# Half-size matmuls of linear attention, head norms and differential scores written as full 128x128 forms

## The chip, the cores and the metric

The kernel runs on one core of one Trainium2 chip. The metric is the device time of one execution in microseconds (us), the median of three runs. A core has a matrix engine (TensorE, PE in the profile, with its weight loads as PEld), VectorE (DVE), ScalarE (ACT), GpSimd (POOL), and SyncE (SP), which issues most of the DMA transfers here. TensorE reads a stationary operand of up to 128 rows (the contraction) and 128 columns (which become the partitions of the result) and streams a moving operand of up to 512 columns through it. A matmul whose contraction has 64 rows, or whose stationary operand has 64 or 32 columns, is called half-size in this text, one of 128 x 128 full.

## The reference, cut to what matters

Two layers of a diffusion backbone on 256 context tokens and 256 latent tokens, 1024 features. In each layer one projection of the normalised input feeds three branches: (A) grouped-query attention with a norm of every head of 64 features, (B) a bidirectional gated linear attention in chunks of 64 tokens, (C) differential attention. Their outputs go through gates into one projection; a gated MLP with a short convolution follows. The second layer gives no context output.

```python
# A: norm of each head of 64 features
qa_l = apply_axial_rope(rms_norm(qa_l, qk_g[0]), cos, sin) * scale
# B: chunks of 64 tokens, once forward and once backward
att = jnp.where(causal, jnp.einsum('bhnid,bhnjd->bhnij', q_d, k_d), 0.0)
o_intra = jnp.einsum('bhnij,bhnje->bhnie', att, v)
o_inter = jnp.einsum('bhncd,bhnde->bhnce', q_d, s_start)
# C: two softmaxes over heads of 64 features
sc = jnp.einsum('bqhmd,bkhmd->bhmqk', qc, kc).astype(jnp.float32)
pc = jax.nn.softmax(sc, axis=-1)
pd = (pc[:, :, 0] - lam * pc[:, :, 1]).astype(vc.dtype)
```

## The kernel before

All large products run on float32 operands split into two halves of the type float32r, a high and a low one; a product is three matmuls (high x high, high x low, low x high). Weights come by DMA into tiles `raw`; ScalarE casts the high half `wh` (L336), VectorE makes the low half `wl` (L338), three tiles of each in rotation. Projections are L350 to L352 (feature-major) and L562 to L564 (token-major), outputs of the MLP and of the branches' sum L467 to L469.

Functions are written as streams: a lead stream (linear attention, then attention A, then C) is woven with a fill stream (values, gates, merges, and in layer 0 the sums L266 of the conditioning) by costs that each step yields. From that the framework makes a fixed order for every engine; each engine works through its own order, and waits where an operand or a buffer is not ready. Two pools of PSUM banks hold results: three `mm` for projections, five `ps` for the rest.

*Values* (`vproj`, L550): 1184 columns in four blocks of 296, for four tiles of 128 tokens, into one tile `V`: the values of B, the decay input, the values of A and of C. Blocks 1 and 0 come ahead of the linear attention, blocks 2 and 3 in its fill.

*Linear attention* (`gla`, L797): for context and latent tokens (g) and four heads (h), 16 passes, of which 12 want an output (all in layer 0, the latent ones in layer 1). The 64 features of a head lie twice on the partitions, forward in 0 to 63, backward in 64 to 127. A pass makes cumulative decays `G` (L850), chunk sums `us` (L856, contraction over the 64 tokens of a chunk), exponentials `ep` and `en` on ScalarE, `en` times the keys on GpSimd (L865), `qd` = `ep` times the queries on VectorE (L867), and then the scores `at` (L876, contraction over 64 features, forward and backward apart), which are masked and added to `as`. The states `ss` are carried from chunk to chunk on VectorE (L894), after GpSimd has cleared or copied their start (L884 to L888). The output `o` of a tile of 128 tokens is one full matmul of `as` with the values (L901) and two of `qd` with a state (L903), each for 64 tokens, so 64 columns of the stationary operand. A norm follows, whose power is GpSimd's (L364). Operands here are float32, not float32r; a float32 matmul leaves two records in the trace.

*Head norms of A* (`head_scale`, L581, ten calls): squares on ScalarE, per token tile a matmul with 32 columns of ones (L587), a copy of its rows (L589), a transposition (L591), and the mean (L593).

*Scores of C* (`attention_c`, L679): a score is two matmuls into one bank. `stacked` (L482) puts the high half of a key head on its 64 partitions and the low half on the other 64; `doubled` (L492) puts the high half of a query head on both. The first matmul contracts over all 128 partitions (high query with both key halves), the second over 64 (low query with high key). Then come the maximum (L723), the exponential (L598), and the difference of the two softmaxes (L732) on VectorE and ScalarE, transpositions (L516) and the product with the values (L700). The scores of A (`attention_a`) are two full matmuls each, of the same shapes.

The functions that the change touches, and what calls them:

## Time and profile before

| | |
|---|---|
| three runs, us | 1602.23, 1603.44, 1605.70 |
| median, us | 1603.44 |
| profiled execution: first to last instruction, us | 1602.8 |
| TensorE busy, us (share) | 1544.4 (96%) |
| VectorE busy | 1018.0 (64%) |
| ScalarE busy | 744.7 (46%) |
| GpSimd busy | 221.7 (14%) |

The profile is one execution. For the profiled execution only its span is known, 0.6 us below the median of the runs. TensorE's busy time has modelled ends: neighbouring matmuls overlap in it, and one of 128 columns shows a duration of 0.27 us though the next may start 0.11 us later. Starts are what can be compared. The chain of work that ended last, and the waits, name TensorE for nearly all of the run. Layer 0 has its linear attention at about 100 to 205 us, attention A to 358, attention C to 530; in layer 1 these stages stand at 1085 to 1170, to 1260, and to 1350.

### The profile page before, as it was taken

To read this page: it belongs to the slowest core of one execution; us is meant where nothing else is said; L and a number is where in the kernel's file an instruction comes from. 1 tells how busy PE (TensorE), PEld (TensorE's weight loads), DVE (VectorE), ACT (ScalarE), POOL (GpSimd) and SP (SyncE) were. 2 spreads that over 40 slices of the span, in tenths; PEclk is the share of its full clock that TensorE was granted. 3 is DMA by queue.
4 is the path that set the end of the run, shared out by engine and by line. 5 is a ranking of instruction groups with operands and counts; after the bars stand their busy time and mean duration, and the time that the engine had idled before them with its cause. 6 is when DMAs were issued, how large, how long until landed. Compare 5 with 4: busy or idle time off the path is not lost. (4 is left out here: it accounts for less than half of the span.)

```text
span 1602.8 us, 25470 instructions
## 1 busy us (share of the span) xinstructions
PE 1544.4 (96%) x9859; PEld 1279.6 (80%) x9859; DVE 1018.0 (64%) x1963; ACT 744.7 (46%) x1330; POOL 221.7 (14%) x284
## 2 busy tenths in 40 slices
PE   7999999999999998999999999899999999899998
PEld 4898767776777887988788777799888878799986
DVE  3636554555667546877787845646667687577754
ACT  3464334453444346533333335655545655465543
POOL 2101110000111223100000223610111122200000
PEclk8999999999999999999999999999999999999999
DMA  9421245215422346644455545432333223665553
GB/s 318 146 88 49 78 149 154 73 54 169 140 60 72 111 134 218 186 149 147 147 157 162 162 128 162 139 109 74 113 125 106 72 74 113 215 205 182 183 191 110
DMA packets 91577, 217.28 MB, mean 136 GB/s; under 512 B 7568, under 2 KB 34832, under 8 KB 91456
## 3 DMA queue, kind: packets, MB, share of 16 engines
q1 hardware_dynamic: 90496, 212.37, 42.2%
q0 software_dynamic: 960, 3.29, 0.7%
q8 instruction: 77, 1.26, 0.3%
q14 instruction: 44, 0.36, 0.1%
HBM read 214.58 MB, written 1.05 MB: 135 GB/s over the span
## 5 line engine op out<-in xcount | busy, mean ns | idle before, releaser
L338 DVE TENSOR_TENSOR wl<-raw,wh 128x1024 fp32r<-128x1024 f32 (+4 forms) x333 | 385.2, 1161 | 223.2 <-ACT wh L336 218.7
L336 ACT CAST wh<-raw 128x1024 fp32r<-128x1024 f32 (+4 forms) x333 | 320.7, 967 | 305.5 <-PE mm L351 146.0
L350 PE MATMUL mm<-act,wh 128*128 128x256 f32 (+1 forms) x1096 | 376.1, 343 | 0.8 <-DVE ft L990 0.7
L352 PE MATMUL mm<-act,wl 128*128 128x256 f32 (+1 forms) x1096 | 371.3, 339 | 1.3 <-DVE wl L338 1.2
L351 PE MATMUL mm<-act,wh 128*128 128x256 f32 (+1 forms) x1096 | 371.1, 339 | 0.4 <-POOL act L398 0.4
L350 PEld LDWEIGHTS mm<-act,wh 128*128 128x128 f32 x1096 | 208.6, 190 | 28.5 <-issue 8.2
L352 PEld LDWEIGHTS mm<-act,wl 128*128 128x128 f32 x1096 | 208.6, 190 | 25.8 <-issue 2.7
L351 PEld LDWEIGHTS mm<-act,wh 128*128 128x128 f32 x1096 | 208.7, 190 | 22.5 <-issue 2.9
L352 PE MATMUL ps<-act,wl 128*128 128x256 f32 (+1 forms) x328 | 109.2, 333 | 0.0
L350 PE MATMUL ps<-act,wh 128*128 128x256 f32 (+1 forms) x328 | 109.1, 333 | 0.0
L351 PE MATMUL ps<-act,wh 128*128 128x256 f32 (+1 forms) x328 | 109.1, 333 | 0.0
L321 DVE SCALAR_TENSOR_TENSOR aacc<-raw,scol,aacc 128x256 f32<-128x256 f32 x224 | 99.1, 505 | 4.5 <-DMA raw<-in_ada 4.5
L469 PE MATMUL ps<-wh,al 128*128 128x512 f32 x198 | 78.9, 398 | 3.3 <-POOL al L1116 3.2
L1116 POOL TENSOR_TENSOR al<-ac,ah 128x256 fp32r<-128x256 f32 x44 | 40.8, 932 | 288.4 <-ACT ah L1115 288.4
L562 PE MATMUL mm<-wh,act 128*128 128x296 f32 x256 | 78.1, 305 | 0.5 <-ACT kb L757 0.5
L563 PE MATMUL mm<-wl,act 128*128 128x296 f32 x256 | 77.2, 301 | 0.3 <-DVE wl L338 0.2
L564 PE MATMUL mm<-wh,act 128*128 128x296 f32 x256 | 76.9, 300 | 0.2 <-POOL act L398 0.2
L352 PEld LDWEIGHTS ps<-act,wl 128*128 128x128 f32 x328 | 62.3, 190 | 6.1 <-DVE wl L338 0.2
L351 PEld LDWEIGHTS ps<-act,wh 128*128 128x128 f32 x328 | 62.4, 190 | 5.9
L350 PEld LDWEIGHTS ps<-act,wh 128*128 128x128 f32 x328 | 62.4, 190 | 5.9
L951 POOL TENSOR_TENSOR acc<-acc,sig 128x512 f32<-128x512 f32 (+1 forms) x32 | 41.7, 1304 | 118.4 <-DVE sig L950 118.4
L364 POOL TENSOR_TENSOR st<-st,mhalf 128x1 f32<-128x1 f32 (+3 forms) x56 | 47.8, 854 | 62.4 <-DVE st L910 35.7
(294 smaller groups left out, 2846.0 us busy)
## 6 DMA issues: line engine op xcount, KB each, us to landing
raw<-in_wflat SPq DMA_DIRECT2D x253, 512.0 KB, 3.6
raw<-in_ada SPq DMA_DIRECT2D x80, 512.0 KB, 3.8
raw<-in_wflat SPq DMA_DIRECT2D x48, 256.0 KB, 2.7
araw<-in_ada SPq DMA_DIRECT2D x32, 256.0 KB, 6.1
raw<-in_wflat SPq DMA_DIRECT2D x16, 444.0 KB, 3.4
raw<-in_wflat SPq DMA_DIRECT2D x8, 384.0 KB, 5.8
raw<-in_wflat SPq DMA_DIRECT2D x8, 296.0 KB, 3.3
xs<-in_ctxt SPq DMA_DIRECT2D x1, 1024.0 KB, 7.9
```

Of the source, the lines that this page charges most:

```text
L321: nc.vector.scalar_tensor_tensor(acc[:, g], r[:, k], s, acc[:, g], ALU.mult, ALU.add)
L336: nc.scalar.copy(h, raw)
L338: nc.vector.tensor_sub(lo, raw, h.bitcast(F32))
L350: self.nc.tensor.matmul(ps, a, xh(k), start=first and k == 0, stop=False)
L351: self.nc.tensor.matmul(ps, a, xl(k), start=False, stop=False)
L352: self.nc.tensor.matmul(ps, b, xh(k), start=False, stop=last and k == nk - 1)
L364: self.nc.gpsimd.tensor_tensor(r, ms, self.mhalf[:, :n], ALU.pow)
L469: self.nc.tensor.matmul(ps, xl, wh, start=False, stop=last)
L562: nc.tensor.matmul(ps, uh[:, k, tt], h[:, c], start=k == 0, stop=False)
L563: nc.tensor.matmul(ps, uh[:, k, tt], lo[:, c], start=False, stop=False)
L564: nc.tensor.matmul(ps, ul[:, k, tt], h[:, c], start=False, stop=k == KD - 1)
L951: nc.gpsimd.tensor_add(acc[:, d, :], acc[:, d, :], s)
```

## The change

Every half-size matmul of three places is written as a full one by zeros in an operand; the contraction or the columns that are added hold zeros and add nothing to the result. Names and lines of the kernel after are those in the diff and the order below (the matmuls L876, L903 and L587 of before are L880, L907 and L590 there, L509 is L511, L546 is L548).

- *Scores of C*: `doubled` makes the low query tile as wide as the high one, and GpSimd clears the 64 partitions of each head that were left out (two memsets a call, 16 in all).
- *Linear attention*: `en` becomes `enm`, with forward and backward in separate columns and zeros on the other 64 partitions; two such tiles, one for each parity of the head, are cleared once a layer. The product with the keys is half GpSimd's and half VectorE's. `qd` is copied by GpSimd into `qdm`, one tile, in which each chunk's 64 columns stand in a tile of 128 with zeros beside (two copies a pass). Chunk sums (L856), and the transpositions of the keys, stay half-size.
- *Head norms*: the squares become the stationary operand, two columns of ones the moving one; the result has tokens on the partitions, so the copy and the transposition go.
- *Values*: one tile for B and the decay input (544 columns), which is given back after the linear attention, and one for A and C (640); the four blocks are 272, 272, 320 and 320 columns wide.

```diff
-VCOLS = 1184
-VBLK = VCOLS // 4
+VW = (272, 272, 320, 320)
+VFROM = (0, 272, 544, 864)
...
     def doubled(self, wk, x, tag, bufs, low_twice):
-        lo = wk.tile([P, 1 + low_twice, x.shape[1]], F32R, tag=f"{tag}l", name=self.nm(tag), bufs=bufs)
+        lo = wk.tile([P, 2, x.shape[1]], F32R, tag=f"{tag}l", name=self.nm(tag), bufs=bufs)
...
                 if o is own or low_twice:
-                    nc.vector.tensor_sub(lo[o, e * low_twice, :], x[own], h[own, e, :].bitcast(F32))
+                    nc.vector.tensor_sub(lo[o, e, :], x[own], h[own, e, :].bitcast(F32))
+                else:
+                    nc.gpsimd.memset(lo[o, e, :].bitcast(F32), 0.0)
...
     def head_scale(self, wk, ps, n):
-            nc.tensor.matmul(bank[32 * t:32 * t + 32, :P], self.C[:, C_HO - C_COS:C_HO - C_COS + 32], sq[:, t * P:(t + 1) * P], start=True, stop=True, skip_group_check=True)
-        rows = self.sm.tile([P, P], F32, tag="arow", name=self.nm("rows"), bufs=2)
-        nc.vector.tensor_copy(rows[:32 * nt], bank[:32 * nt, :P])
-        st = bank[:, P:P + 32 * nt]
-        nc.tensor.transpose(st, rows[:32 * nt], self.ident[:32 * nt, :32 * nt])
+            nc.tensor.matmul(bank[:, 2 * t:2 * t + 2], sq[:, t * P:(t + 1) * P], self.C[:, C_HO - C_COS:C_HO - C_COS + 2], start=True, stop=True, skip_group_check=True)
...
     def attention_c(self, l, wk, u, V, yC, q0, nq):
-                    s = self.scores([(qh[:, e, cq], ks[:, e, :nk]), (ql[own, 0, cq], ks[own, e, :nk])])
+                    s = self.scores([(x[:, e, cq], ks[:, e, :nk]) for x in (qh, ql)])
...
     def gla(self, l, wk, ek, V, decay, Q, K, gs, yB, full, q0):
-        for x in atm:
-            for y in x:
-                nc.gpsimd.memset(y, 0.0)
+        enm = [wk.tile([P, 2, 2 * P], F32, tag=f"enm{i}", name=self.nm("enm")) for i in range(2)]
+        qdm = wk.tile([P, 2, 2, P], F32, tag="qdm", name=self.nm("qdm"))
+        for x in (*atm[0], *atm[1], *enm, qdm):
+            nc.gpsimd.memset(x, 0.0)
...
-                    en = one("en")
-                    for r, c in halves:
-                        nc.scalar.activation(p2(en)[r], G[r, :, c], AF.Exp, scale=-1.0)
-                    nc.gpsimd.tensor_mul(en, en, K[h // 2][:, h % 2, g * CTX:(g + 1) * CTX])
+                    em = enm[h % 2]
+                    for s, (r, c) in enumerate(halves):
+                        nc.scalar.activation(p2(em[:, s])[r], G[r, :, c], AF.Exp, scale=-1.0)
+                    for s, eng in enumerate((nc.gpsimd, nc.vector)):
+                        r = halves[s][0]
+                        eng.tensor_mul(em[r, s, :], em[r, s, :], K[h // 2][r, h % 2, g * CTX:(g + 1) * CTX])
                     qd = one("qd")
                     nc.vector.tensor_mul(qd, ep, Q[h // 2][:, h % 2, g * CTX - q0:(g + 1) * CTX - q0])
+                    for ci in range(2):
+                        c = slice(CH * ci, CH * ci + CH)
+                        nc.gpsimd.tensor_copy(qdm[:, ci, :, c], p2(qd)[:, :, c])
...
-                            r = slice(HD * s, HD * s + HD)
-                            nc.tensor.matmul(at[s][:, tl(t)], en[r, tl(t)], qd[r, tl(t)], start=True, stop=True, skip_group_check=True)
+                            nc.tensor.matmul(at[s][:, tl(t)], em[:, s, tl(t)], qd[:, tl(t)], start=True, stop=True, skip_group_check=True)
...
-                        nc.tensor.matmul(o[CH * ci:CH * ci + CH, t, :], qd[:, t * P + CH * ci:t * P + CH * ci + CH], ss[:, 2 * t + ci, :],
-                                         start=False, stop=ci == 1, skip_group_check=True)
+                        nc.tensor.matmul(o[:, t, :], qdm[:, ci, t, :], ss[:, 2 * t + ci, :], start=False, stop=ci == 1, skip_group_check=True)
...
     def layer(self, l, u, finish):
-            V = right.enter_context(pool("v", far)).tile([P, 4, VCOLS], F32, name=self.nm("V"))
+            V = [st.enter_context(pool(n, side)).tile([P, 4, w], F32, name=self.nm(n)) for st, n, side, w in ((gst, "vb", near, 2 * VW[0]), (right, "va", far, 2 * VW[2]))]
```

Where the order of instructions moves. First TensorE in a pass of the linear attention of layer 0, the output of the second token tile and the chunk sums of the next pass. Before:

```order
L903 MATMUL ps_1538<-ss_1625,qd_1556 64x128 x2
L901 MATMUL ps_1538<-V_734,as_1623 128x128
L903 MATMUL ps_1538<-ss_1625,qd_1556 64x128 x2
L856 MATMUL ps_1674<-V_734,ke_1086 128x128 x2
L351 MATMUL mm_1652<-act_111,wh_1655 128x512
```

After:

```order
L907 MATMUL ps_1554<-ss_1643,qdm_1044 128x128 x2
L905 MATMUL ps_1554<-vb_734,as_1641 128x128
L907 MATMUL ps_1554<-ss_1643,qdm_1044 128x128 x2
L856 MATMUL ps_1692<-vb_734,ke_1096 128x128 x2
L351 MATMUL mm_1670<-act_111,wh_1673 128x512
```

The order is the same; the results of the state matmuls have 128 partitions instead of 64, and `qdm` stands for `qd`. In attention C the order of TensorE is the same line by line.

Second, GpSimd's queue in the first passes of the linear attention of layer 0. Before, products with the keys (`en`), starts of the states (`ss`) and powers of the norms (`st`):

```order
L865 TENSOR_TENSOR en_1146<-en_1146,kb_707 128x256
L865 TENSOR_TENSOR en_1280<-en_1280,kb_707 128x256
L884 MEMSET ss_1485 64x128
L885 MEMSET ss_1485 64x128
L364 TENSOR_TENSOR st_1262<-st_1260,mhalf 128x2
L865 TENSOR_TENSOR en_1420<-en_1420,kb_712 128x256
L884 MEMSET ss_1625 64x128
L885 MEMSET ss_1625 64x128
L364 TENSOR_TENSOR st_1376<-st_1374,mhalf 128x2
```

After:

```order
L867 TENSOR_TENSOR enm_1042<-enm_1042,kb_707 64x256
L872 COPY qdm_1044<-qd_1160 128x2x64 x2
L867 TENSOR_TENSOR enm_1043<-enm_1043,kb_707 64x256
L872 COPY qdm_1044<-qd_1296 128x2x64 x2
L888 MEMSET ss_1501 64x128
L889 MEMSET ss_1501 64x128
L364 TENSOR_TENSOR st_1274<-st_1272,mhalf 128x2
L867 TENSOR_TENSOR enm_1042<-enm_1042,kb_712 64x256
L888 MEMSET ss_1643 64x128
L872 COPY qdm_1044<-qd_1438 128x2x64 x2
L889 MEMSET ss_1643 64x128
L364 TENSOR_TENSOR st_1390<-st_1388,mhalf 128x2
```

Two copies into `qdm` now stand behind each product with the keys, and those of the second pass stand ahead of the power of the first pass's norm.

Third, GpSimd's queue at the layer boundary: the clearing of layer 1's tiles, and the statistics of the end of layer 0 (L427 and L364 for two tiles of tokens). Before:

```order
L806 MEMSET atm_10179 128x256
L806 MEMSET atm_10180 128x256
L884 MEMSET ss_10328 64x128
L885 MEMSET ss_10328 64x128
L884 MEMSET ss_10379 64x128
L885 MEMSET ss_10379 64x128
L427 TENSOR_SCALAR st_9718<-st_8342 128x1
L364 TENSOR_TENSOR st_9720<-st_9718,mhalf 128x1
L427 TENSOR_SCALAR st_9723<-st_8344 128x1
```

After:

```order
L806 MEMSET atm_10203 128x256
L806 MEMSET atm_10204 128x256
L806 MEMSET enm_10205 128x512
L806 MEMSET enm_10206 128x512
L427 TENSOR_SCALAR st_9738<-st_8362 128x1
L806 MEMSET qdm_10207 128x512
L364 TENSOR_TENSOR st_9740<-st_9738,mhalf 128x1
L888 MEMSET ss_10358 64x128
L889 MEMSET ss_10358 64x128
L888 MEMSET ss_10409 64x128
L889 MEMSET ss_10409 64x128
L427 TENSOR_SCALAR st_9743<-st_8364 128x1
```

Three memsets of 512 columns are added, two ahead of the first L427 and one behind it; the small memsets `ss` have moved from ahead of the first L427 to ahead of the second.

## Rows read from the trace of the kernel before

**Rows 1.** Page: the span; busy us (share) x instructions; granted clock in tenths by slice.

```profile
span 1602.8 us, 25470 instructions
...
PE 1544.4 (96%) x9859; PEld 1279.6 (80%) x9859; DVE 1018.0 (64%) x1963; ACT 744.7 (46%) x1330; POOL 221.7 (14%) x284
...
PEclk8999999999999999999999999999999999999999
```

**Rows 2.** Waits: engine, tile, line <- releaser: total us, times, longest.

```profile
ACT wh L336 <- PE mm L351: 146.0, 66, 4.6
...
PE ps L266 <- DMA araw<-in_ada: 10.9, 4, 5.4
PE ps L391 <- ACT hn L380: 6.4, 2, 4.0
```

**Rows 3.** Timeline, TensorE, attention C, layer 0: start us, us, engine, line, operands, records.

```profile
430.78 1.75 PE L509 MATMUL ps<-ks,q 128*128 128x512 f32 x4
432.47 0.50 PE L350 MATMUL mm<-act,wh 128*128 128x512 f32 x1
432.80 0.40 PE L351 MATMUL mm<-act,wh 128*128 128x512 f32 x1
```

**Rows 4.** Timeline, TensorE, attention C, layer 1 (the six alternate full and half).

```profile
1270.23 2.54 PE L509 MATMUL ps<-ks,q 128*128 128x512 f32 x6
1272.70 0.50 PE L352 MATMUL mm<-act,wl 128*128 128x512 f32 x1
1273.04 0.28 PE L350 MATMUL mm<-act,wh 128*128 128x256 f32 x1
```

**Rows 5.** Timeline, TensorE, attention A, layer 0, full scores.

```profile
251.78 0.63 PE L509 MATMUL ps<-k,qs 128*128 128x512 f32 x2
252.25 0.39 PE L350 MATMUL mm<-act,wh 128*128 128x512 f32 x1
```

**Rows 6.** Groups by line and form: half-size scores of C with 512 keys.

```profile
L509 PE MATMUL ps<-ks,q 64*128 64x512 f32 x32 | 15.9, 496 | 0.1
```

**Rows 7.** Timeline, TensorE, linear attention, layer 0, one pass.

```profile
121.81 0.71 PE L876 MATMUL ps<-qd,en 64*128 64x128 f32 x8
122.46 0.39 PE L850 MATMUL ps<-tri,gh 128*128 128x256 f32 x1
122.68 0.28 PE L850 MATMUL ps<-tri,gl 128*128 128x256 f32 x1
...
126.22 0.44 PE L903 MATMUL ps<-ss,qd 128*64 128x128 f32 x4
...
127.38 0.48 PE L856 MATMUL ps<-V,ke 64*128 64x128 f32 x2
```

**Rows 8.** Timeline, TensorE, full float32 records, attention C, layer 0.

```profile
462.42 1.05 PE L700 MATMUL ps<-V,pt 128*128 128x128 f32 x8
...
463.54 0.39 PE L350 MATMUL mm<-yA,wh 128*128 128x512 f32 x1
```

**Rows 9.** Head norms: group L587; timeline and durations (ns, min/median/max) of L811.

```profile
L587 PE MATMUL ps<-sq,C 128*32 128x128 f32 x64 | 4.2, 285 | 1.1 <-ACT sq L584 1.1
...
103.65 0.46 PE L811 MATMUL ps<-ident,kb 64*128 64x64 f32 x4
...
L811 PE MATMUL ps<-ident,kb x32: 221/223/273, 103.7 to 1088.1; 64*128 64x64 f32 x32
```

**Rows 10.** GpSimd: group of state copies; timeline at the layer boundary.

```profile
L887 POOL COPY ss<-carry 64x128 f32<-64x128 f32 x8 | 2.7, 336 | 43.6 <-PE ps L903 35.4 <-DVE carry L894 8.2
...
1021.65 1.08 POOL L806 MEMSET atm<- 128x256 f32 x4
...
1023.70 0.30 POOL L427 TENSOR_SCALAR st<-st 128x1 f32<-128x1 f32 x1
...
1024.75 2.44 POOL L427 TENSOR_SCALAR st<-st 128x1 f32<-128x1 f32 x1
```

**Rows 11.** Stretch of attention C, layer 1: us, busy us (records) by engine, clock, DMA.

```profile
1262.00:1345.00 83.00, 77.24 (x487) 63.75 (x486) 68.39 (x158) 46.80 (x97) 16.20 (x19) 1.00 0.30 91
```

More of the change, by code (lines that the diff above doesn't have):

```diff
@@ L99, in pack_weights @@
                                    np.arange(OFF["va"], OFF["va"] + 128), np.arange(OFF["vc"], OFF["vc"] + 512)])
-            cols = cols[key[2] * VBLK:(key[2] + 1) * VBLK]
+            cols = cols[VFROM[key[2]]:VFROM[key[2]] + VW[key[2]]]
             a = wi[VK[key[3]][0] * P:VK[key[3]][1] * P][:, cols]
@@ L555, in vproj @@
             ws = [self.weights((l, "v", b, i)) for i in range(len(VK))]
+            n = VW[b]
             for t in tiles:
-                ps = self.mm()[:, :VBLK]
+                ps = self.mm()[:, :n]
                 for k in range(KD):
                     h, lo = ws[k // 3]
-                    c = slice((k % 3) * VBLK, (k % 3 + 1) * VBLK)
+                    c = slice((k % 3) * n, (k % 3 + 1) * n)
                     tt = slice(t * P, (t + 1) * P)
@@ L564, in vproj @@
                     nc.tensor.matmul(ps, ul[:, k, tt], h[:, c], start=False, stop=k == KD - 1)
-                nc.scalar.copy(V[:, t, b * VBLK:(b + 1) * VBLK], ps)
+                nc.scalar.copy(V[b // 2][:, t, b % 2 * n:(b % 2 + 1) * n], ps)
                 yield 3000
@@ L719, in attention_c @@
                 for e in range(2):
-                    own, cq = slice(HD * e, HD * e + HD), slice(q * P, (q + 1) * P)
-                    s = self.scores([(qh[:, e, cq], ks[:, e, :nk]), (ql[own, 0, cq], ks[own, e, :nk])])
+                    cq = slice(q * P, (q + 1) * P)
+                    s = self.scores([(x[:, e, cq], ks[:, e, :nk]) for x in (qh, ql)])
                     mx = self.st(1)
@@ L1037, in layer @@
                 run(self.vproj(l, u, V, (0,)))
-                decay = self.gla_decay(l, ek, V)
+                decay = self.gla_decay(l, ek, V[0])
             pre = iter(()) if l else self.gates_b(l, u, gs, (2, 3), q0, nq)
             ada = lambda r: self.ada_units(l, r) if full else iter(())
-            self.weave(self.gla(l, wk, ek, V, decay, q2, k2, gs, yB, full, q0), chain(pre, self.vproj(l, u, V, (2, 3)), self.gates(l, sp, u, 4 * T // nq, q0, nq)), (1.3, 1.4)[l])
+            self.weave(self.gla(l, wk, ek, V[0], decay, q2, k2, gs, yB, full, q0), chain(pre, self.vproj(l, u, V, (2, 3)), self.gates(l, sp, u, 4 * T // nq, q0, nq)), (1.3, 1.4)[l])
             gst.close()
```

12 lines of the change are left out of this document (6 added, 6 removed).

## The prediction

> **What bounds the kernel now.** I read the page first. TensorE is busy 96% of a span of 1602.8 us, and its clock row stands at 9 in every slice but the first, which is the upper level of 2.4 GHz [rows 1]. A busy TensorE need not be an efficient one, so I went to the waits next. ScalarE waits 146 us for TensorE to give back the weight tiles that it casts, while TensorE's own longest wait in total is 10.9 us for the first weights [rows 2]: TensorE sets the pace nearly everywhere, and a shorter TensorE instruction shortens the run unless something new becomes late. Then I read the timeline, and there the starts of neighbouring rows, not their durations: matmuls overlap, so the price of one is the distance from its start to the next start.
>
> That distance shows the price of a change of form. In grouped-query attention both matmuls of a score are full, and two of them take 0.47 us, 0.235 each [rows 5]. In differential attention every second one contracts over 64 rows. Four of these take 1.69 us from 430.78 to 432.47, and the full matmul behind them 0.33 instead of 0.235: 2.02 where five full ones would take 1.18, 0.42 too much for each pair [rows 3]. Six in layer 1 take 2.47, and the next one 0.34: 2.81 against 7 x 0.235 = 1.65, 0.39 for each pair [rows 4]. A half-size matmul streams the same columns as a full one, so the excess is that of going to the half form and back. I take 0.40 a pair, 0.20 for each switch of form, part of which falls on the matmul before the switch and part on the one behind it.
>
> **The change part by part.** *Differential scores.* The low query half gets 64 rows of zeros, so both matmuls are full. Layer 0 has 4 heads x 4 query tiles x 2 = 32 half-size matmuls [rows 6], layer 1 has 4 x 2 x 2 = 16. TensorE saves 48 x 0.40 = 19.2 us. The columns stay the same, and in this stage the order of instructions is the same as before, so no wait is moved by the order itself.
>
> *Linear attention.* In each of 12 head passes that produce an output, four score matmuls (L876) and four state matmuls (L903) become full. In float32 each of them leaves two records. Half-size ones run two at a time: eight records of L876 take 0.65 us from 121.81 to 122.46, of which about 0.20 is the switching, 0.45/8 = 0.056 a record; the first full matmul behind them again takes 0.22 [rows 7]. Full float32 records cannot share: eight of L700 and one matmul of 512 columns take 1.12 us, so (1.12 - 0.235)/8 = 0.111 a record [rows 8]. 12 x 16 = 192 records x (0.111 - 0.056) = 10.6 us more. Against this stand the switches: counted along TensorE's order with these two as full forms, 65 fall away (six a pass, less the places where a neighbour such as L856 stays half-size), 65 x 0.20 = 13.0. Net 2.4 us saved. One pass as a check: L903, L901, L903 take 1.16 from 126.22 to 127.38 [rows 7], and ten full records would take 1.11.
>
> *Head norms.* Ten calls of the helper lose their 32-column matmuls, a VectorE copy and a transposition; 28 switches go, 5.6 us. The 64 records of L587 occupy 4.2 us with ten tails of 0.28, so some 1.4 [rows 9]; the ten transpositions 10 x 0.111 = 1.1. New are 64 records that load 128 columns of weights and stream two. The trace has none of these; the nearest row is L811, which also loads 128 columns and streams 64: (0.46 - 0.22)/3 = 0.08 [rows 9], where 0.22 is the tail of one. 64 x 0.08 = 5.1, so 5.6 + 2.5 - 5.1 = 3.0 saved; with 0.056 a record it is 4.5, with 0.111 it is 1.0. The Trainium skill, "TensorEngine Tiling (Array Packing)", section Performance Considerations, puts a floor of about 60 cycles under any matmul, an estimate of 0.025 us and 6.5 us saved; its "TensorE: Matmul & The Clock Gate", section LDWEIGHTS, has a load of 128 columns take 128/1.2 = 107 ns, which would leave 1.3. The spacing of L811 lies between them, and I stay with the row.
>
> *Values' split.* Blocks of 296 columns become 272, 272, 320, 320. The sum of columns is the same, about 2 us a layer move from ahead of the linear attention into its fill, where TensorE is as busy. Nothing.
>
> TensorE's sum: 19.2 + 2.4 + 3.0 = 24.6 us saved.
>
> **What is given back.** *Layer 1's differential attention*: in 1262 to 1345 us TensorE is busy 77.2 of 83 us and VectorE 68.4 [rows 11]; there the softmax and the rotation on VectorE come close to setting the pace, so of 16 x 0.40 = 6.4 us I take half as lost, 3.2 (between none and 6.4). In layer 0 the filling matmuls are twice as wide and cover the chain: 1.0 (none to 4). *GpSimd in the linear attention*: each pass gains two copies ahead of the state copies and of the power of the next norm. A copy of the same length is 0.336 us [rows 10]: 24 x 0.336 = 8.1 if all is exposed, none if the fill covers it; the half of the key product that moves to VectorE stands in its queue ahead of weight halves that TensorE has three tiles in stock of. I take 2.0 for both, near the lower end, since GpSimd is nearly idle there. *Layer boundary*: three memsets of 512 columns now stand ahead of the statistics (L427) of the feed-forward's end. Four of 256 take 1.08 us, and behind four small ones the first L427 follows without a gap [rows 10]; TensorE waits 4.0 us for the result of this chain [rows 2]. 3 x 0.54 = 1.6, all exposed. The 16 memsets of the query halves lie on an idle queue: nothing, or 2 us if they hold up a rotation.
>
> Given back: 3.2 + 1.0 + 2.0 + 1.6 = 7.8. So 24.6 - 7.8 = 16.8 us saved. The profiled span of 1602.8 becomes 1586.0; the median of the runs lies 0.6 above the span, so I forecast 1586.6 us.
>
> **The rivals.** *All of it comes through*: nothing new is late; 1603.4 - 24.6 = 1578.8. For it: TensorE hardly waits anywhere [rows 2].
> *The softmax chain sets the pace in differential attention*: layer 1 gives back all 6.4 and layer 0 half of its 12.8; with the other 3.6 the saving is 24.6 - 16.4 = 8.2, 1595. For it speaks VectorE's 82% in layer 1 [rows 11]; against it that six score matmuls in a row run without a gap [rows 4].
> *Work done two at a time was worth more than the switching.* The 10.6 us are paid, but the neighbours in the linear attention are half-size too, and the 13.0 don't come: 24.6 - 13.0 - 7.8 = 3.8, 1599.6. The Trainium skill, "TensorEngine Tiling (Array Packing)", sections Theoretical Speedup and Key Properties, speaks for this one: small tiles run independently, up to twice as fast, and only a change of mode drains the array. The pairs of L876 agree with the first half [rows 7]; the counted order has the switches, so I give it little.
> *Slower*: GpSimd becomes the bound of the linear attention. One L427 on a single column took 2.44 us where the one before it took 0.30 [rows 10]; if the 24 copies stretch like that, a pass has 4.9 us of them in a queue that the norm's power stands behind. It turns the sum from 24.6/12 = 2.05 us of TensorE's wait a pass; with 2.9 a pass, 35 us, the time is 1614.
> *The change doesn't do what it says*: if the low half's matmul is slow for another reason than its form (its operand, its bank), the 19.2 stay, and the rest cancels with what is given back: 1603.
>
> **How the numbers follow.** Forecast 0.58, all comes through 0.17, softmax chain 0.10, two at a time 0.07, slower 0.04, no effect 0.04. The time is the first case's. The range runs from 1578 (all of it) to 1597 (the softmax chain with the GpSimd term doubled) and leaves out the last three cases and some of the tails. A difference of 0.2%, 3.2 us, is about what can be told from none: faster than 1600.2 are the first three cases and half of the fourth, 0.89; within it 0.06; slower 0.05.
>
> **What the profile will show.** If I am right, the score rows of differential attention stand 0.23 us apart and the full matmul behind them is no longer longer; this alone makes layer 0's stage some 12 us shorter. The linear attention keeps its length within 4 us, with its records of both lines 0.11 us apart. L546 and the first scores of a head in layer 1 wait a little longer than now. At the layer boundary TensorE waits 1 to 2 us longer. I am wrong if the pairs keep their 0.42, if TensorE shows waits on the copied queries (the state matmuls held by GpSimd), or if VectorE in layer 1 reaches 90%.

## The result and the profile after

Four runs of the changed kernel have a median of 1593.51 us (1593.17 to 1595.1), those of the kernel before, beside them, 1603.51 (1602.23 to 1605.7): a ratio of 0.9939, with a 95% interval of 0.9922 to 0.9955. The change saves 10.0 us. The forecast was 1586.6 us, in a range of 1578 to 1597. So the sign and the range held, and the saving is 6.8 us smaller than forecast.

The page of the changed kernel, in the parts that answer to [rows 1]:

```profile
span 1591.1 us, 25543 instructions
...
PE 1527.7 (96%) x9849; PEld 1292.1 (81%) x9849; DVE 1022.8 (64%) x1965; ACT 744.4 (47%) x1330; POOL 238.0 (15%) x330
```

TensorE is busy for the same share, 16.7 us less of a span that is 11.7 us shorter: some of what it saved became idle time. The waits of the changed kernel (engine, tile, line <- releaser: total us, times, longest), to be set beside [rows 2]:

```profile
PE ps L391 <- ACT hn L380: 7.0, 2, 4.6
PE ps L548 <- DVE on L539: 6.3, 6, 1.9
...
PE ps L639 <- DVE pt L523: 2.3, 4, 1.0
```

The kernel before waited 6.4, 3.5 and 0.4 us in these three places (the lines there are L391, L546 and L640); of the rise in the second, 1.9 us stood before under another releaser of the same matmul. The first is the layer boundary, the second the output norm of differential attention, the third the product of probabilities and values in attention A, which the forecast did not name.

**Differential scores.** Timeline of TensorE, layer 0 and layer 1 (start us, us, engine, line, operands, records), to be set beside [rows 3, 4]:

```profile
428.63 1.17 PE L511 MATMUL ps<-ks,q 128*128 128x512 f32 x4
429.64 0.39 PE L350 MATMUL mm<-act,wh 128*128 128x512 f32 x1
429.86 0.39 PE L351 MATMUL mm<-act,wh 128*128 128x512 f32 x1
...
1260.74 1.66 PE L511 MATMUL ps<-ks,q 128*128 128x512 f32 x6
1262.24 0.39 PE L352 MATMUL mm<-act,wl 128*128 128x512 f32 x1
1262.47 0.28 PE L350 MATMUL mm<-act,wh 128*128 128x256 f32 x1
```

Four scores and the full matmul behind them take 1.23 us where they took 2.02, which is 0.395 a pair; six and the one behind them 1.73 instead of 2.81, 0.36 a pair. The 32 matmuls of [rows 6] are 16 of each layer, those with 512 keys; the other 16 of layer 0 have 256, as a further group of the kernel before shows (line, engine, operands, records, busy us, mean ns):

```profile
L509 PE MATMUL ps<-ks,q 64*128 64x256 f32 x16 | 6.1, 381 | 0.0
```

Over all scores, each block taken up to the second start behind it, a pair saves 0.39 us in layer 0 with 512 keys, 0.34 with 256, and 0.33 in layer 1: 11.7 and 5.3 us in all. The next rows are the first and the last scores of the stage, in layer 0 and in layer 1, in the changed kernel:

```profile
379.52 0.64 PE L511 MATMUL ps<-ks,q 128*128 128x256 f32 x4
...
506.92 0.71 PE L511 MATMUL ps<-ks,q 128*128 128x512 f32 x2
...
1259.88 0.73 PE L511 MATMUL ps<-ks,q 128*128 128x512 f32 x2 [0.61 <-ACT q L500]
...
1322.40 0.70 PE L511 MATMUL ps<-ks,q 128*128 128x512 f32 x2
```

Layer 0's stage is 127.4 us from first to last; in the kernel before the same scores start at 378.03 and 516.01, 138.0. That is 10.6 saved. Layer 1's is 62.5 instead of 65.5 (1269.04 to 1334.57), 3.0 saved, of the 5.3 that its 16 pairs are worth. The stretch of the changed kernel that answers to [rows 11]:

```profile
1253.00:1333.00 80.00, 72.09 (x485) 63.82 (x485) 68.14 (x157) 46.66 (x96) 18.21 (x25) 1.00 0.31 93
```

VectorE's work stayed (68.1 us), TensorE's fell by 5.2, and TensorE's idle time rose from 5.8 to 7.9 us: VectorE is now at 85% and TensorE at 90%.

**Linear attention.** One pass in the changed kernel, beside [rows 7]:

```profile
121.34 1.09 PE L880 MATMUL ps<-qd,enm 128*128 128x128 f32 x8
122.18 0.39 PE L567 MATMUL mm<-wh,act 128*128 128x320 f32 x1
...
125.27 0.31 PE L565 MATMUL mm<-wh,act 128*128 128x320 f32 x1
125.62 0.68 PE L907 MATMUL ps<-ss,qdm 128*128 128x128 f32 x4
126.14 0.39 PE L905 MATMUL ps<-vb,as 128*128 128x128 f32 x2
126.36 0.61 PE L907 MATMUL ps<-ss,qdm 128*128 128x128 f32 x4
126.90 0.71 PE L856 MATMUL ps<-vb,ke 64*128 64x128 f32 x4
```

Eight records of the first product start 0.105 us apart (0.84 / 8) in this pass, 0.101 in the other eleven (0.81 / 8, where the half-size ones took 0.65). The block of L907 and L905 takes 1.28 us from 125.62 to 126.90, where the half-size one took 1.16. This is one of the two dearest blocks: over the twelve passes the block takes 1.06 to 1.28 us, 14.0 in sum, against 13.9 before; 1.21 and more are passes in which a half-size matmul stands beside it. The matmul of 320 columns ahead of the block is followed after 0.35 us, where it streams for 0.15: TensorE waits there. What for is seen in layer 1, in VectorE's last states of a pass and TensorE's first products with them, in the kernel before and in the changed one:

```profile
1137.14 1.11 DVE L894 SCALAR_TENSOR_TENSOR ss<-ss,ep,ps 64x128 f32<-64x128 f32 x3
...
1138.31 0.44 PE L903 MATMUL ps<-ss,qd 128*64 128x128 f32 x4
...
1128.95 0.72 DVE L898 SCALAR_TENSOR_TENSOR ss<-ss,ep,ps 64x128 f32<-64x128 f32 x2
...
1129.82 0.68 PE L907 MATMUL ps<-ss,qdm 128*128 128x128 f32 x4
```

The states end at 1138.25 and 1129.67, and the products start 0.06 and 0.15 us behind them. Before, seven of the twelve passes start within 0.08 us of the last state; in the changed kernel ten load the operand 0.11 to 0.12 us behind it. In these passes VectorE's states set the start, so the change of form ahead of the products lay in a wait, and without it nothing is gained there. The copies into `qdm` end 3.7 us or more ahead of the products that read them.

**Head norms.** One call of the kernel before (two pieces: its products, and in layer 1 the transposition of its rows), and then the same call of the changed kernel:

```profile
277.03 0.40 PE L351 MATMUL mm<-yB,wh 128*128 128x512 f32 x1
277.36 0.43 PE L587 MATMUL ps<-sq,C 128*32 128x128 f32 x8
277.71 0.50 PE L352 MATMUL mm<-yB,wl 128*128 128x512 f32 x1
278.05 0.39 PE L350 MATMUL mm<-act,wh 128*128 128x512 f32 x1
...
1190.13 0.28 PE L350 MATMUL mm<-act,wh 128*128 128x256 f32 x1
1190.35 0.27 PE L591 MATMUL ps<-ident,rows 64*128 64x64 f32 x1
...
1190.77 0.28 PE L352 MATMUL mm<-act,wl 128*128 128x256 f32 x1
```

```profile
278.16 1.05 PE L590 MATMUL ps<-C,sq 128*128 128x2 f32 x8
279.08 0.48 PE L351 MATMUL mm<-yB,wh 128*128 128x512 f32 x1
279.39 0.40 PE L352 MATMUL mm<-yB,wl 128*128 128x512 f32 x1
```

Eight old records and their two full neighbours take 1.02 us (277.03 to 278.05); two such neighbours alone are 0.47, so the records with both switches cost 0.55, and the transposition 0.11 more in layer 0. Eight new records take 0.92 to the next start, 0.115 each, and the next matmul is 0.08 longer than its 0.23: 1.00 against 0.66. Over the ten calls the 64 new records take 7.0 us, 0.110 each, with calls from 0.09 to 0.12. In layer 1 a query call has four records, and its transposition is of 64 rows, a half form: 0.64 us for two matmuls of 0.12 and itself, so 0.40. There the new call is the cheaper one. With six calls of eight records and four of four, TensorE itself loses some 6 x 0.34 and gains 4 x 0.3 to 0.4, an estimate from these two calls.

**Layer boundary.** GpSimd's queue in the changed kernel, beside [rows 10]:

```profile
1013.27 1.01 POOL L806 MEMSET enm<- 128x512 f32 x2
1014.39 0.30 POOL L427 TENSOR_SCALAR st<-st 128x1 f32<-128x1 f32 x1
1014.74 0.52 POOL L806 MEMSET qdm<- 128x512 f32 x1
```

The three new memsets take 1.5 us, but the four small ones that stood ahead of the first L427 have moved behind it, as the order showed. From the first memset of `atm` to the first L364 the queue takes 2.98 us (1012.26 to 1015.24) where it took 2.44 before. What TensorE waits for at this place (L391 for L380) rose by 0.6 us, from 6.4 to 7.0. The experiments below bear the link out: in e7, with `enm` alone, the queue takes 2.66 us and the wait is 6.6, in e8, with `qdm` alone, 2.91 and 6.9; in e4 and e11, with neither, the wait is 6.4.

### The profile page after: what moved, and what is told of

It is laid out like the page before. It is cut to its first block, busy times and chain, and to the rows that moved or that the text cites. A ratio compares the mean times of both kernels' runs of the same rounds, so it can differ in the third digit from the quotient of the medians.

```text
span 1591.1 us, 25543 instructions
## 1 busy us (share of the span) xinstructions
PE 1527.7 (96%) x9849; PEld 1292.1 (81%) x9849; DVE 1022.8 (64%) x1965; ACT 744.4 (47%) x1330; POOL 238.0 (15%) x330
## 3 DMA queue, kind: packets, MB, share of 16 engines
HBM read 214.58 MB, written 1.05 MB: 136 GB/s over the span
## 5 line engine op out<-in xcount | busy, mean ns | idle before, releaser
L338 DVE TENSOR_TENSOR wl<-raw,wh 128x1024 fp32r<-128x1024 f32 (+6 forms) x333 | 384.6, 1159 | 215.7 <-ACT wh L336 213.0
L336 ACT CAST wh<-raw 128x1024 fp32r<-128x1024 f32 (+6 forms) x333 | 320.7, 967 | 302.6 <-PE mm L351 142.7
L565 PE MATMUL mm<-wh,act 128*128 128x272 f32 (+1 forms) x256 | 77.8, 304 | 1.3 <-ACT kb L756 1.3
L567 PE MATMUL mm<-wh,act 128*128 128x272 f32 (+1 forms) x256 | 77.0, 301 | 0.3 <-POOL act L398 0.3
L566 PE MATMUL mm<-wl,act 128*128 128x272 f32 (+1 forms) x256 | 76.9, 300 | 0.3 <-DVE wl L338 0.3
L364 POOL TENSOR_TENSOR st<-st,mhalf 128x1 f32<-128x1 f32 (+3 forms) x56 | 47.3, 845 | 177.6 <-DVE st L592 144.2
```

Source lines behind the costliest of these rows:

```text
L336: nc.scalar.copy(h, raw)
L338: nc.vector.tensor_sub(lo, raw, h.bitcast(F32))
L364: self.nc.gpsimd.tensor_tensor(r, ms, self.mhalf[:, :n], ALU.pow)
L565: nc.tensor.matmul(ps, uh[:, k, tt], h[:, c], start=k == 0, stop=False)
L566: nc.tensor.matmul(ps, uh[:, k, tt], lo[:, c], start=False, stop=False)
L567: nc.tensor.matmul(ps, ul[:, k, tt], h[:, c], start=False, stop=k == KD - 1)
```

## The experiments

All runs of a row of labels stand beside runs of the kernel before on the same chip: median 1603.3 us for e1 to e4, 1603.5 for e5 to e8, 1604.8 for e9 to e12. Stage lengths are differences of starts on TensorE in the profiled run, as above. Where no fall of the clock meets them, profiles of an unchanged stage (linear attention, attention A, scores of C) agree within 0.15 us, while medians of the same kernel on different chips differ by up to 1.7 us (1593.5 and 1595.2 for the changed one).

**e1: the scores alone.**

```diff
-        lo = wk.tile([P, 1 + low_twice, x.shape[1]], F32R, ...)
+        lo = wk.tile([P, 2, x.shape[1]], F32R, ...)
...
+                    nc.gpsimd.memset(lo[o, e, :].bitcast(F32), 0.0)
...
-                    s = self.scores([(qh[:, e, cq], ks[:, e, :nk]), (ql[own, 0, cq], ks[own, e, :nk])])
+                    s = self.scores([(x[:, e, cq], ks[:, e, :nk]) for x in (qh, ql)])
```

> The kernel before with the change of the differential scores alone (zeros in the low query half, both matmuls of a score full); everything else as before. My theory: a switch of form costs TensorE 0.20 us, 48 pairs hold some 93 of them, so 18 to 19 us of TensorE's time go, and some 4 to 5 come back as waits, most in layer 1: 13 to 14 us faster than before (1590), which is more than the whole change gave (10). Rival: the parts need each other or the gain of this part is lost to the softmax chain: 8 us or less.

Measured: 1589.14 us (1588.17 to 1590.74), ratio 0.991 [0.9896, 0.9925], 14.2 us saved. The stage is 127.3 us in layer 0 and 62.6 in layer 1, as in the whole change, and the other stages are those of the kernel before. That is just above what the theory gave, and the rival is refuted. The scores alone save more than the whole change: the rest of it costs about 4 us.

**e2: the head norms alone.**

```diff
-            nc.tensor.matmul(bank[32 * t:32 * t + 32, :P], self.C[:, C_HO - C_COS:C_HO - C_COS + 32], sq[:, t * P:(t + 1) * P], ...)
+            nc.tensor.matmul(bank[:, 2 * t:2 * t + 2], sq[:, t * P:(t + 1) * P], self.C[:, C_HO - C_COS:C_HO - C_COS + 2], ...)
```

> The kernel before with the head norms' change alone (squares as the stationary operand, two moving columns, no copy, no transposition). The trace of after shows a spacing of 0.11 us for a matmul of two columns, where I had taken 0.08. My theory: 28 switches and 2.5 us of old records go (8.1 us), 64 records x 0.112 = 7.2 come, so TensorE's time is 1 us shorter and the rest is what the new order of the work behind it makes late: 1602.5, between -1 and +2 us against before. Rival, the prediction's term: 3 us faster (1600.5).

Measured: 1607.67 us (1602.18 to 1611.05), ratio 1.0023 [1.0011, 1.0034]: a loss of 4.4 by the medians, outside the theory's range (up to 2) and against the rival's sign. Attention A of layer 0 (first score to last product with the values) is 127.2 us long, 124.9 before; in layer 1 61.2 instead of 61.4, and the stretch ahead of it 40.3 instead of 41.4. Other stretches that the change reaches add 0.9. Together the norms cost 2.0 us by stages; the other 2.4 of the median are not shown to be theirs. TensorE has waits that are not in the kernel before, first in its waits here:

```profile
PE ps L636 <- DVE pt L521: 2.4, 4, 1.0
```

VectorE shows where they come from. Its rows and GpSimd's ahead of the first of these waits, in the kernel before and then in e2 (the number in brackets is idle time and what ended it):

```profile
278.90 0.70 DVE L478 TENSOR_TENSOR rt<-sh,C 128x256 f32<-128x256 f32 x1
...
281.13 0.17 DVE L628 TENSOR_SCALAR st<-st 128x8 f32<-128x8 f32 x1 [0.39 <-POOL st L364]
...
278.59 0.73 POOL L479 TENSOR_TENSOR qx<-qx,C 128x256 f32<-128x256 f32 x1 [36.43 <-DVE sh L476]
279.28 1.82 POOL L364 TENSOR_TENSOR st<-st,mhalf 128x8 f32<-128x8 f32 x1
```

```profile
280.04 0.69 DVE L624 TENSOR_SCALAR st<-st 128x8 f32<-128x8 f32 x1 [1.45 <-POOL st L364]
...
282.38 0.41 DVE L478 TENSOR_TENSOR rt<-sh,C 128x256 f32<-128x256 f32 x1
...
278.37 1.64 POOL L364 TENSOR_TENSOR st<-st,mhalf 128x8 f32<-128x8 f32 x1 [37.04 <-DVE st L589]
279.97 0.74 POOL L479 TENSOR_TENSOR qx<-qx,C 128x256 f32<-128x256 f32 x1
```

Before, the long chain of the norm (copy, transposition) let the rotation (L476 to L480) go first, and GpSimd's power (L364) ran behind it. The new chain is shorter, so the fixed order puts the power ahead of the rotation's product on GpSimd, and the scaling that waits for it (L624, L628 before) ahead of the rotation on VectorE. VectorE stands idle 1.45 us, and copies of transposed probabilities come late: in attention A of layer 0 two products with the values (L636) wait for them, 0.7 us for L521 and 0.2 for L519.

**e5: the same, with the rotation written ahead of the norm.**

```diff
         def prepare(m):
             ps = self.uproj((l, "qa", m), u, q0, q0 + nq)
-            rq = self.head_scale(wk, ps, nq)
-            sc = self.st(2 * nqt)
-            nc.vector.tensor_scalar_mul(sc, rq, HD ** -0.5)
             qx = wk.tile(...)
...
             self.rope(wk, qx[:, nq - SEQ:])
+            rq = self.head_scale(wk, ps, nq)
+            sc = self.st(2 * nqt)
+            nc.vector.tensor_scalar_mul(sc, rq, HD ** -0.5)
```

> Head norms alone, as in e2_norms_only, but the queries' rotation is written ahead of their norm, so that VectorE meets the rotation's products before the scaling of the statistics that waits for GpSimd's power (in e2 it stood idle 1.45 us there, and two copies of the transposed probabilities came 0.74 and 0.42 us late for TensorE). Theory order (the norms lose because the shorter chain of statistics moves GpSimd's power and VectorE's scaling ahead of the rotation): TensorE's waits in the first layer's attention A go back from 4.0 to about 2.3 us and in the second's from 5.0 to about 3, and the kernel runs at 1603 to 1605 us, 2 to 4 us under e2's 1607.7. Rival price (the norms lose by what TensorE spends: 64 more weight loads of 128 columns at 0.112 us): the waits and the time stay at e2's, 1606 to 1609 us.

Measured: 1605.53 us (1603.26 to 1609.98), ratio 1.0011 [1.0001, 1.0021]. Attention A of layer 0 is 126.0 us, 1.2 less than in e2, and its waits for the copies (L636 for L521 and L519) are gone there. So the order makes about half of the loss of 2.3 us in this stage; the 1.1 that are left agree with three calls of the stage at 1.00 instead of 0.66, TensorE's own. In layer 1 the order gains nothing: 1.3 us of waits for L521 stay (1.7 in e2), attention A takes 61.3 us (61.2), and the stretch ahead of it is 41.4 again, where e2 had 40.3. Over all stretches that the norms reach, e5 is 0.5 us shorter than e2. Its time of 1605.5 lies between the two theories, 2.1 under e2, on another chip and with intervals that overlap: that the order is worth more than these 0.5 us is not shown.

**e6: 32 moving columns instead of 2.**

```diff
-            nc.tensor.matmul(bank[:, 2 * t:2 * t + 2], sq[...], self.C[:, C_HO - C_COS:C_HO - C_COS + 2], ...)
+            nc.tensor.matmul(bank[:, 32 * t:32 * t + 32], sq[...], self.C[:, C_HO - C_COS:C_HO - C_COS + 32], ...)
```

> Head norms alone, each product with 32 moving columns instead of 2 (the 30 more results are not read). Theory load (the 128-column stationary operand sets the pace): the records of these products stay 0.112 us apart, as with two columns. Rival columns (a fixed part and then the columns): clearly over 0.112, 0.15 or more. Theory small (what I took in the forecast: 0.08 us for a short product) is already against the two-column records and would need them below 0.1 here.

```profile
276.56 1.08 PE L587 MATMUL ps<-C,sq 128*128 128x32 f32 x8
277.47 0.48 PE L351 MATMUL mm<-yB,wh 128*128 128x512 f32 x1
```

Eight records take 0.91 us, 0.114 each, with 16 times the columns, and call by call the spacing is that of e2: the columns don't set the pace. There is one run of e6, whose time is not used. Full float32 records of 128 columns are as far apart, 0.111 [rows 8]. What these have in common is a stationary operand of 128 columns.

**e3, e4, e7, e8: linear attention.** e4 has the values' split alone; e3 the split with all of the linear attention's change; e7 the split and the first products full; e8 the split and the products with the states full.

```diff
 e7
-                            nc.tensor.matmul(at[s][:, tl(t)], en[r, tl(t)], qd[r, tl(t)], ...)
+                            nc.tensor.matmul(at[s][:, tl(t)], em[:, s, tl(t)], qd[:, tl(t)], ...)
 e8
-                        nc.tensor.matmul(o[CH * ci:CH * ci + CH, t, :], qd[:, t * P + CH * ci:t * P + CH * ci + CH], ss[:, 2 * t + ci, :], ...)
+                        nc.tensor.matmul(o[:, t, :], qdm[:, ci, t, :], ss[:, 2 * t + ci, :], ...)
```

> The kernel before with the linear attention's change and the split of the values, without the scores' and the norms' changes. My theory, from the stages of the two traces: the switches that go (about 13 us) are paid by records that no longer run two at a time (about 11) and by waits on GpSimd and VectorE of 2 to 4 us: within -1 and +3 us of before. Rival, the prediction's terms: 2.4 saved, 2.0 given back, so 0; a second rival, that GpSimd's copies hold up the state matmuls in every pass: over 5 us slower.

> The kernel before with the values' split alone (two tiles, blocks of 272, 272, 320, 320 columns). Both theories: no change, within 1.5 us of before; if it is slower by more, part of what the whole change gave back is the split's (another place of the tiles in memory, other waits for it, values' columns moved into the fill of the linear attention).

> Of the linear attention's change only the first products (keys by queries, L880 after) are full, with the values' split; the products with the states stay half-size. Theory of the sum: 96 records go from 0.056 to 0.111 us (+5.3 us), some 24 to 30 changes of array form go (-4.8 to -6.0 us): within 1 us of the split alone (1604.1), 1603 to 1606 us. Rival GpSimd (the split of the keys' product between GpSimd and VectorE delays TensorE): waits in the first layer's linear attention rise from 2.3 to over 3.5 us and the time to 1607 or more.

> Of the linear attention's change only the products with the states (L907 after) are full, with their operand copied into zeroed places by GpSimd, and the values' split; the first products stay half-size. Theory of the sum: +5.3 us for 96 records, -4.8 to -6.0 us for changes of form: 1603 to 1606 us. Rival GpSimd (the copies into the zeroed operand make TensorE wait): the waits before these products, about 0.3 us three times in the second layer's linear attention in the changed kernel, come with this part alone, and the time is 1606 to 1609 us, over e7's by 2 us or more.

| | time, us (median) | ratio, interval | stage, layer 0, us | stage, layer 1, us |
|---|---|---|---|---|
| before | | | 77.2 | 55.8 |
| e4 split | 1604.10 | 1.0009 [0.9996, 1.0021] | 79.2 | 57.0 |
| e7 first products | 1606.74 | 1.0023 [1.0012, 1.0034] | 79.8 | 57.1 |
| e8 state products | 1604.78 | 1.0007 [0.9993, 1.0021] | 79.2 | 57.2 |
| e3 both | 1608.71 | 1.0029 [1.0018, 1.0039] | 79.6 | 57.3 |

The stage runs from the first to the last product of the chunk sums (L856), so the last pass's own products lie behind it. The split lengthens it by 2.0 and 1.2 us and gives about as much back ahead of it (in layer 0 the stage starts 2.5 us sooner, a part of which is the clock: from 12 to 28 us it is at 0.68 in the profile of before and at 1.00 in e4's), and its time can't be told from none. Either product, or both, changes the stage by 0.6 us or less against e4; behind the stage, up to the first score of attention A, e3 is 0.4 us longer than e4 in layer 0 and 0.15 in layer 1. The linear attention's change costs 1.3 us by these stretches: unshared records and dropped switches nearly cancel. GpSimd does not hold TensorE: in the changed kernel one wait of 0.2 us for VectorE's states (L907 for L898) is all that the list of waits has in layer 0, and the copies into `qdm` end long before.

The times say more than the stages. e8 is in its theory's range, e7 0.7 us above its own, and e3, 5.4 us over the kernel before, is where only the rival of the copies had it, though the waits of that rival are not there. e3 is 4.6 us over e4 by the medians. The profile of e3 shows where 2.7 us lie, in a stretch that the edit does not touch. Its granted clock in layer 1's differential attention, in e3 (stretch, us, busy us and records of PE, PEld, DVE, ACT, POOL, clock, DMA):

```profile
1288.00:1292.00 4.00, 2.98 (x12) 1.52 (x10) 2.81 (x9) 2.77 (x6) 0.00 (x0) 0.98 0.00 0
1292.00:1296.00 4.00, 4.00 (x11) 2.32 (x10) 2.73 (x8) 3.07 (x6) 0.97 (x1) 0.50 0.47 131
```

After a wait of 1.0 us at 1289.56 the clock goes to 0.50, which is 1.2 of 2.4 GHz, for about seven us, and that stage, here up to its very last score, is 68.65 us long where it is 65.9 in the kernel before, in e4, e7 and e8. So part of what parts cost alone is a clock that falls after a wait. Ten of e3's twelve runs are over 1606 us, but so are eight of e2's, which leaves the linear attention as it was, three of e4's, and one of the 29 of the kernel before beside them: that the linear attention's change makes such falls more frequent is not shown.

**e9, e10, e11: the whole, and the whole without one part.** e9 is the changed kernel again; e10 has the old head norms, e11 the old linear attention.

```diff
 e10
-            nc.tensor.matmul(bank[:, 2 * t:2 * t + 2], sq[...], self.C[...], ...)
+            nc.tensor.matmul(bank[32 * t:32 * t + 32, :P], self.C[...], sq[...], ...)
 e11
-                            nc.tensor.matmul(at[s][:, tl(t)], em[:, s, tl(t)], qd[:, tl(t)], ...)
+                            nc.tensor.matmul(at[s][:, tl(t)], en[r, tl(t)], qd[r, tl(t)], ...)
```

> The changed kernel once more, beside its variants on one chip. The parts alone gave -14.2 us (scores), +3.7 to 4.4 (norms) and +4.6 to 5.4 (linear attention with the split) against the kernel before: added up, 1597 to 1598 us. Theory addition: the whole comes out there, and the 1593.5 of the first measurement was low. Rival (parts share losses, so that the whole loses less than its parts): 1593 to 1594.5 us again.

> The changed kernel with the old head norms (scores, linear attention and split changed). Addition: 1603.4 - 14.2 + 4.6 = 1593.8 us, which is 3.7 us under the whole if the norms cost in it what they cost alone. Rival (norms pay here, as I forecast, 3.0 us): 1 to 3 us over the whole.

> The changed kernel with the old linear attention (scores, norms and split changed). Addition: 1603.4 - 14.2 + 3.7 + 0.6 = 1593.5 us, some 4 us under the whole of the same chip. Rival (linear attention pays here, as I forecast, 0.4 us net of GpSimd's part): equal to the whole or a little over.

Measured: e9 1595.18 us (1592.13 to 1595.31), ratio 0.9934 [0.9922, 0.9947]; e10 1594.13, 0.9933 [0.992, 0.9945]; e11 1590.11, 0.991 [0.9896, 0.9923]. All five runs of e9 lie under the plain addition of the parts (1597 to 1598), and its median 0.7 above the rival's range; the kernel before is 1.4 us slower on this chip. The norms cost 1.05 us in the whole by the medians (e9 less e10), where addition had 3.7 and the rival a gain; the intervals can't tell it from nothing; attention A of layer 0 shows its 2.3 (127.2 against 124.9 in e10) and the stretch ahead of it in layer 1 gives 1.0 back. The linear attention costs 5.1 by the medians, more than addition gave, and with it gone the kernel is as fast as the scores alone. The profiles place most of that. Of the 4.9 us between the profiled executions of e9 and e11, 1.8 lie in its stages (0.4 and 0.3) and behind them (0.9 and 0.15), and 3.1 in two stretches that it does not touch, where e9's clock stood lower: attention C of layer 0, and the end of layer 1. First the changed kernel and e9, one and the same kernel, in attention C of layer 0, then e9 and e11 at the end:

```profile
379.52:507.23 127.71, 123.19 (x739) 97.63 (x738) 91.16 (x221) 59.56 (x122) 21.23 (x23) 1.00 0.35 111
...
379.78:508.82 129.04, 124.70 (x740) 98.91 (x738) 91.47 (x221) 59.65 (x122) 21.23 (x23) 0.99 0.33 108
...
1338.59:1593.18 254.59, 239.72 (x1722) 220.69 (x1720) 158.79 (x223) 126.01 (x195) 19.52 (x27) 0.98 0.53 178
...
1335.21:1588.24 253.03, 237.78 (x1722) 219.30 (x1720) 158.69 (x223) 126.08 (x195) 20.39 (x27) 0.99 0.53 179
```

The clock column, the third from the end, is lower in the longer row of each pair. In e11 attention C takes 127.5 us, as in the first row. At the end 254.4 and 254.6 us stand in the kernel before and in e1 too, which have the old linear attention, so the 1.6 us there are not the edit's.

**e12: the scores, with zeros that are written once.**

```diff
+        low = [wk.tile([P, 2, nq], F32R, tag=f"low{i}", name=self.nm("low")) for i in range(2)]
+        for x in low:
+            nc.gpsimd.memset(x.bitcast(F32), 0.0)
...
-                else:
-                    nc.gpsimd.memset(lo[o, e, :].bitcast(F32), 0.0)
...
-            return ks, *self.doubled(wk, qx, "q", 2, False)
+            return ks, *self.doubled(wk, qx, "q", 2, False, low[m % 2])
```

> Scores' change alone as in e1_scores_only, with the low halves in two tiles that are zeroed once a layer instead of one cleared by GpSimd at each of the 8 preparations. In e1 TensorE waited 0.41 us once in the second layer for GpSimd's clearing; its other new waits there (about 2.2 us in all) are for VectorE. Theory (softmax chain on VectorE gives the layer-1 gain back): only that wait goes, 1588.5 to 1589.2 us, with the second layer's stretch at 62.4 to 62.9 us. Rival (GpSimd's clearing, which also holds up the rotation's products on its queue, is behind the other waits too): the stretch falls to 61 us or under and the time to 1587.5 or under.

Measured: 1590.38 us (1587.8 to 1591.21), ratio 0.9904 [0.9889, 0.992]. Layer 1's stage is 62.5 us (62.6 in e1), without any wait for GpSimd's clearing; the time is 1.2 us above the theory's range, on a chip on which the kernel before is 1.5 us slower. The clearing was not what gives the gain back there; the waits that are left are for VectorE and ScalarE. e1 and e12 are the fastest kernels of the study, faster than both the kernel before and the changed one, and can't be told from each other or from e11.

## Why the prediction held in sign and range, and where it was too high

| term of the sum | forecast, us | measured, us |
|---|---|---|
| scores, layer 0 (12.8 less 1.0) | 11.8 saved | 10.6 saved |
| scores, layer 1 (6.4 less 3.2) | 3.2 saved | 3.0 saved |
| linear attention (2.4 less 2.0 for GpSimd) | 0.4 saved | 1.3 lost, 0.7 in its stages, 0.6 behind them |
| values' split | nothing | nothing that can be told |
| head norms | 3.0 saved | 2.0 lost (e2, by stages), 1.05 (e10, by medians) |
| layer boundary | 1.6 lost | 0.6 lost |
| sum | 16.8 saved | 9.7 saved by stages; 10.0 by the times |

The measured column comes from stage lengths in profiles whose stages show no fall of the clock (the changed kernel, e1, e2 in attention A, e3 and e4 in the linear attention), and, for the boundary, from its wait; the sum of it agrees with the times. The sign and the range rest on the scores alone: the other parts, forecast to save 1.8 us, cost 3.9.

*Scores: right.* The price of a switch, 0.20 us each, holds for layer 0 with 512 keys; it is 0.17 with 256 keys and in layer 1. Layer 1 gives back 2.3 of 5.3 us, nearly the half that was forecast, and most of it where the forecast said, to VectorE: in its stretch of the changed kernel L548 waits 2.7 us for L539 instead of 1.8, and the transposition L518 0.6 instead of 0.2, both for VectorE; another 0.7 of L548 is put down to ScalarE (L336), and e12 shows that GpSimd's clearing has no part in it. This also answers the rival of the softmax chain: not quite half is given back in layer 1, and a tenth in layer 0 (1.1 of 11.7).

*Head norms: the mis-sized term.* The step that failed is the price of a record that streams two columns. I took 0.08 us, the spacing of L811 [rows 9], which is half-size in its rows; such records share the array, which is probably why they start so close. The measured mean is 0.110 (7.0 us for 64), close to the upper end that I gave (0.111), and e6 shows that the moving columns have no part in it, since 16 times as many change nothing. The Trainium skill, "TensorE: Matmul & The Clock Gate", section LDWEIGHTS, puts a load of 128 columns at 128/1.2 = 107 ns; the mean of the trace agrees with it within 3%. 7.0 - 5.1 = 1.9 us of the miss of 5.0 are this. More is on the old side and in the order: in layer 0 an old call cost 0.66 us, less than the 0.81 that the forecast's terms give it (5.6 and 2.5 over ten calls), and the forecast looked for no wait in attention A, where VectorE then waits for GpSimd ahead of the rotation. e5 shows that this wait is a matter of order in layer 0, worth 1.2 us there. Some 1 us is not placed.

*Linear attention: the switches were overrated.* Full records start 0.10 to 0.115 us apart, as taken, and switches fall away; but they pay a little less than the records cost, where the forecast had 2.4 us left over. The block that the forecast used as its check comes out at 1.11 us or less in seven of the twelve passes, as forecast, and at 1.21 to 1.28 where a half-size matmul stands beside it. What the sum of the switches left out is the wait ahead of the block: the first product with a state starts right behind VectorE's last state in seven passes before and ten after, so there the switch was worth nothing. The rival that work done two at a time was worth more than the switching is not borne out by the stages, which would have to be some 10 us longer in all. The rival of the slower GpSimd is refuted, its copies are done in time. Of the 4.6 and 5.1 us by which the medians of e3 and e9 exceed those of e4 and e11, the profiles put 2.7 and 3.1 on the clock in stretches that the edit does not touch; whether the edit has a part in how often the clock falls stays open.

*Layer boundary: right in place, too large.* The three memsets stand in the queue, but the small ones that moved behind the first L427 make room for them: of 1.5 us, 0.5 are left ahead of the first L364.

## What to carry to other kernels

Filling an operand with zeros pays where a half-size matmul stands alone between full ones: it costs two changes of form, 0.33 to 0.40 us here, and the full form streams the same columns. Where half-size float32 matmuls come in groups, they share the array (0.056 us a record against 0.10 to 0.11), and full ones only trade that for the switches. A change that shortens a side chain changes the order in which a scheduler places its steps on the other engines; look at what then stands ahead of the work that TensorE waits for, and try the urgent chain first: here it brought 1.2 us back in one stage of layer 0 and nothing in layer 1.

## What the runs showed of the hardware

A product with two moving columns and one with 32 take the same 0.114 to 0.115 us in the call shown when the stationary operand has 128 columns, and the same 0.10 to 0.12 in the others.

The small scaling of the norms on VectorE (128 x 8 or 128 x 4) takes 0.17 us in seven of its eight places in the kernel before and 0.69 to 0.71 in seven of eight in e2. The one shown starts at 280.04 us, just as GpSimd's 0.74 us product of the rotation (L479) starts at 279.97, and ends with that product. Such a product runs beside all seven long ones of e2 and beside the one long one of the kernel before (0.70 us at 1192.29), and beside none of the short ones; in e5, where the two no longer meet, all eight take 0.17.

TensorE's clock can fall to 1.2 GHz after a short wait, and does not always do so at the same place. The changed kernel and e9 are one kernel: TensorE waits 1.94 us up to 502.5 us in both, and the clock falls behind it in e9 alone (the rows of attention C above, 129.0 against 127.7 us). In e5 and in the kernel before it waits 1.93 us up to 510.5 us in the same way; the stretch behind it is at 1.00 in the kernel before and here, in e5, at half:

```profile
514.00:518.00 4.00, 4.00 (x9) 1.87 (x8) 1.70 (x5) 1.05 (x3) 0.00 (x0) 0.50 0.00 0
518.00:522.00 4.00, 4.00 (x12) 2.78 (x12) 0.59 (x2) 1.73 (x4) 0.00 (x0) 0.52 0.00 0
```

It makes that stage 142.4 us instead of 138.4, 4 us that belong to no edit. Such falls go with the scatter of single runs here (1602 to 1612 us for e2 to e4): over the 29 runs of the kernel before beside e1 to e4, a run's time and its mean granted clock have a correlation of -0.73, over the 29 beside e5 to e8 -0.79, and in e2, e3 and e4 -0.77, -0.82 and -0.92. It is a reason to compare stages and not only times.
